# Weight buffers moved to multiples of 512 bytes, and layer 1's expert router fed with rows that are not yet normalised

## The chip, the core and the metric

The kernel is one program on one core of a Trainium2 chip. The metric is device time in microseconds (us) of one execution; lower is better. The profiles come from the hardware profiler of one execution.

## The reference, cut to what matters

Two layers over 256 latent rows and 256 context rows of 1024 columns. Each layer normalises, runs three token mixers, merges them, and then sends every row through a mixture of 32 experts. The layer that matters here is the second (`last`), where only the 256 latent rows are left:

```python
x = layer_norm(DEEPNORM_ALPHA * x + g1 * y_lat, ln1_g[l], ln1_b[l])
h = layer_norm0(x) * (1.0 + sc2) + sh2                     # modulate(x, sh2, sc2)
g_logits = h @ w_rg + b_rg                                 # 4 groups
e_logits = h @ w_re + b_re                                 # 32 experts
# top-1 group, top-2 experts in it, gates from two softmaxes
y = sum over the two experts of gate * ((silu(h @ w1[e]) * (h @ w3[e])) @ w2[e])
x = layer_norm(DEEPNORM_ALPHA * x + g2 * y, ln2_g[l], ln2_b[l])
```

`layer_norm0(x)` is `(x - mean) * r` with `r = 1/sqrt(var + eps)`. All is float32. An expert's three matrices are 6 MiB, so a layer's experts are 201 MB that have to come from HBM once.

## The kernel before, in words

Rows stand in tiles of 128: four tiles in layer 0, two in layer 1 (`T`). The order of the instructions on each engine is made by a list scheduler from the program order (an earlier line has the higher priority; `with self.later(n)` puts a block off by n places).

**Buffers.** SBUF is cut into pools that stand behind one another in each partition. From the left: constants and small tiles (`cp`, `sm`, `lp`), then `wp` (18 buffers of 4 KiB: `raw`, `whi`, `wlo`, `h4`), `rp` (what the router keeps), and then a pool that changes with the stage: `mg` for the mixers, `eg` for the experts, which has six buffers of 8 KiB (tag `ew`) for expert weights. From the right end: `mp` for the mixers and, in its place, `ep` for the experts, which has five more buffers of 8 KiB in layer 1 and three in layer 0 (`ewb`). Four pairs of 4 KiB buffers of `wp` serve in layer 1 as further expert buffers (`self.spare`), so the ring there has 6 + 4 + 5 = 15 places of 1 MiB over all partitions. In the compiled program of before, the first byte of the `wp` buffers lies 128 past a multiple of 512, of the `eg` buffers 64 past one, of all in the right-hand pools 480 past one. One row of a transfer goes to one partition; a weight transfer has 128 rows of 8 KiB, or of 4 KiB into a half of a spare pair.

**Between the merges and the experts** (`out_norm`). The sum of the three branches is split into two float32r parts (`yh`, `yl`) and multiplied by `w_out` (`wo`, 48 matmuls for a tile of rows). Tile by tile follow `norm1` (the first layer norm, which gives `x1`), then `norm2`: `norm0` (mean and variance by `bn_stats` on VectorE, L300, then one ScalarE pass, L320), `logits` (eight PE transposes, L1162; eight modulating copies of 128x128, L1168 on ScalarE and L1170 on VectorE; eight matmuls with the router's 36 columns, L1172) and `top2` on VectorE (from L1211 on). `h2_done` transposes the modulated rows back (L1137) and splits them into `h2hi` and `h2lo` (L817, L818). In layer 1 `h2_done` of the last tile stands behind `route` (`LAST[1]` is 0).

**The experts.** `route` makes slots out of the choices; `one_hot` makes the matrices `OH`, `O1`; `gather_T` multiplies the `h2` parts by `OH` (L1395) and copies the result to `XT` (L1397); `body` multiplies `XT` by `w1` and `w3` (L1525), `tail` by `w2` (L1425), `combine` adds up. Expert weights are loaded on SyncE's queue (L1487) in the order in which they are used. The first six loads of a layer stand behind `left.close()`: they overlay `mg`, whose last readers are the `wo` matmuls. The `ewb` loads overlay `mp`, whose last reader in layer 1 is the `h2_done` behind `route`.

Of the kernel before, what the change touches and what calls it, by code (L numbers as in the profile page):

```python
# [10 lines left out]
F32 = mybir.dt.float32  # L11
F32R = mybir.dt.float32r
# [3 lines left out]
AF = mybir.ActivationFunctionType  # L16
ALU = mybir.AluOpType
# [6 lines left out]
EPS = 1e-6  # L24
# [66 lines left out]
QUICK = (4, 2)  # L91
WARM = 0, 8
HB = (), ()
LAST = 1, 0
NE2 = 3, 2
NC2 = 0, 3
NCT = 2, 2
# [152 lines left out]
class _Prog:  # L250
# [808 lines left out]
    def row(self, ap, tag):  # L1059
        r = self.t([128, 1024], tag, name="row")  # L1060
        self.nc.sync.dma_start(r, ap.to_broadcast([128, 1024]))
        return r

    def out_norm(self, l, T, src):

        nc = self.nc
        nq = 128 * T
        yh, yl = [], []
        for dp in range(4):
            h, lo = self.t([128, 2, 512], "h4", F32R, "yh"), self.t([128, 2, 512], "h4", F32R, "yl")  # L1070
            y = self.y[dp][:, :, :nq]
            nc.scalar.activation(h[:, :, :nq], y, AF.Copy, scale=0.5)
            nc.vector.scalar_tensor_tensor(lo[:, :, :nq], y, 0.5, h[:, :, :nq].bitcast(F32), op0=ALU.mult, op1=ALU.subtract)
            yh.append(h)
            yl.append(lo)
        u, g1 = [], {}
        for t in range(T):
            x = self.t([128, 1024], "o4", name="u")
            nc.sync.dma_start(x, src[t])
            nc.scalar.activation(x, x, AF.Copy, scale=ALPHA)  # L1080
            u.append(x)
        early, late = ("o4", "y4") if l else ("y4", "y4")
        if l:
            g1[0] = self.mod_row(l, "g1", 0, early)
            lg = self.row(self.a["ln"][l, 0:1, :], early)
        first, total = {}, {}
        self.x1 = []

        def norm1(t):
            self.x1.append(self.t([128, 1024], "raw", name="x1"))  # L1090
            if t >= T - QUICK[l]:
                total[t] = self.norm_quick(u[t], self.x1[t], lg, lb)
                first[t] = lambda: None
            else:
                first[t] = self.norm(u[t], u[t], lg, lb, self.x1[t])

        def norm2(t):
            first[t]()
            h = self.t([128, 1024], "o4", name="h2")
            self.norm0(self.x1[t], h, total[t] if t in QS[l] else None)  # L1100
            self.logits(l, t, h)

        w = {(h, q): self.piece(l, ("wo", h, q), ("whi", "wlo") if 2 * q + h < NW[l] else ("g4", "g4")) for q in range(4) for h in range(2)}
        for s in range(len(g1), T // 2):
            g1[s] = self.mod_row(l, "g1", s, late)
            if s == 0:
                lg = self.row(self.a["ln"][l, 0:1, :], late)
        lb = self.row(self.a["ln"][l, 1:2, :], late)
        for t in range(T):
            ts = slice(128 * t, 128 * t + 128)  # L1110
            for h in range(2):
                p = self.ps("wo")
                for k in range(8):
                    s = slice(512 * (k % 2), 512 * (k % 2) + 512)
                    self.mm3(p, yh[k // 2][:, k % 2, ts], yl[k // 2][:, k % 2, ts], w[h, k // 2][0][:, s], w[h, k // 2][1][:, s], k == 0, k == 7)
                hs = slice(512 * h, 512 * h + 512)
                tmp = self.t([128, 512], "b2", name="tmp")
                nc.vector.tensor_tensor(tmp, p, g1[t // 2][:, hs], op=ALU.mult)
                (nc.vector if t >= T - QUICK[l] else nc.gpsimd).tensor_tensor(u[t][:, hs], u[t][:, hs], tmp, op=ALU.add)
            norm1(t)  # L1120
            norm2(t)
            if t % 2 and t < T - 1:
                self.top2(l, t - 1, t + 1, T)
            if t:
                self.h2_done(l, t - 1)
        if LAST[l]:
            self.h2_done(l, T - 1)
        self.top2(l, T - 2, T, T)

# [18 lines left out]
    def logits(self, l, t, h):  # L1148
# [22 lines left out]
        for k in range(8):  # L1171
            mm(self.pl[:, 36 * t:36 * t + 36], hT[:, k], self.wr[:, 36 * k:36 * k + 36], start=k == 0, stop=k == 7)  # L1172

    def warm(self, n, x, name="warm"):

        w = x.shape[-1]
        p = self.ps(name)
        with self.later(5000):
            for i in range(n):
                self.nc.tensor.matmul(p[:w, :256], x, self.c["iota"], start=True, stop=True)  # L1180


    def top2(self, l, t0, t1, T):

        nc, c = self.nc, self.c
        TT, TS, STT, RED = nc.vector.tensor_tensor, nc.vector.tensor_scalar, nc.vector.scalar_tensor_tensor, nc.vector.tensor_reduce
        if t0 == 0:
            self.brt = self.t([128, 36], "u1", name="brt")
            nc.sync.dma_start(self.brt, self.a["brt"][l:l + 1, :].to_broadcast([128, 36]))
            x = self.t([128, 1024], "whi", name="route")  # L1190
            self.lg, self.oh = x[:, 0:144], x[:, 144:400]
            g = self.rp.tile([128, 3, T], F32, name=f"gates{l}", tag="gates")
            self.gt = [g[:, i] for i in range(3)]

            self.g2p = self.rp.tile([128, T, 2], F32R, name=f"g2p{l}", tag="g2p")
            self.gdp = self.rp.tile([128, T, 3], BF, name=f"gdp{l}", tag="gdp")
            self.scr, self.scr2 = [x[:, 512 + 128 * i:640 + 128 * i] for i in range(2)], x[:, 768:1024]
            self.M = self.t([128, 32 * T], "u1", BF, "M")
        n = t1 - t0
        lg = self.lg[:, 36 * t0:36 * t1].rearrange("p (t e) -> p t e", e=36)  # L1200

        def row(x, w):
            return x[:, None, :].to_broadcast([128, n, w])
# [4 lines left out]
        def tiles(x):  # L1208
            return x[:, 32 * t0:32 * t1].rearrange("p (t e) -> p t e", e=32)

        TT(lg, self.pl[:, 36 * t0:36 * t1].rearrange("p (t e) -> p t e", e=36), row(self.brt, 36), op=ALU.add)  # L1211

        def mark(oh, x, m, weights, w, op=ALU.is_equal):

# [20 lines left out]
        with self.later():  # L1235
# [12 lines left out]
            p, q = self.g2p[:, t0:t1], self.gdp[:, t0:t1]  # L1248
# [132 lines left out]
        for t in range(T):  # L1381
            mm(p[:, 2:5], O1[:, t], self.gdp[:, t], start=t == 0, stop=t == T - 1)

    def gather_T(self, OH, w, T):

        nc, mm = self.nc, self.nc.tensor.matmul
        XT = self.t([128, 8, w], "e8", name="XT")
        per = 512 // w
        for i in range(0, 8, per):
            p = self.ps("XT")  # L1390
            for j in range(per):
                k = i + j
                for t in range(T):
                    for part in range(2):
                        mm(p[:, w * j:w * j + w], self.h2s[t][part][:, 128 * k:128 * k + 128], OH[:, t], start=t == 0 and part == 0,  # L1395
                           stop=t == T - 1 and part == 1)
            (nc.scalar.copy if (i // per) % 2 else nc.vector.tensor_copy)(XT[:, i:i + per], p.rearrange("p (a b) -> p a b", b=w))  # L1397
        return XT

# [89 lines left out]
    def experts(self, l, T):  # L1489
        nc, mm, c = self.nc, self.nc.tensor.matmul, self.c  # L1490
# [5 lines left out]
        XTs, gates, CY, held = {}, {}, {}, {}  # L1496

        def front(dp):
            d = self.slot
            if dp:  # L1500
                d = self.small(2 * T)
                nc.vector.tensor_scalar(d, self.slot, -256.0 * dp, None, op0=ALU.add)
            OH, O1 = self.one_hot(c["iota"], 256, T, d)
            XTs[dp] = self.gather_T(OH, 256, T)
            pg = self.ps("gate")
            for pr in range(2):
                ss = slice(128 * pr, 128 * pr + 128)
                self.slot_gates(pg[:, 8 * pr:8 * pr + 5], OH[:, :, ss], O1[:, :, ss], T)
            gates[dp] = self.small(2)
            nc.vector.tensor_reduce(gates[dp], pg[:, 0:16].rearrange("p (a b) -> p a b", a=2)[:, :, 0:5], axis=AX.X, op=ALU.add)  # L1510
            CY[dp] = []
# [44 lines left out]
    def overflow(self, l, T):  # L1556

        nc, mm, c = self.nc, self.nc.tensor.matmul, self.c
# [8 lines left out]
        with self.tc.For_i(0, nblk, 1):  # L1567
            sel, eq, row = self.small(1), self.small(16), self.small(1)
# [10 lines left out]
            nc.vector.tensor_scalar(sel, cnt, 128.0, None, op0=ALU.mult)  # L1579
            nc.vector.tensor_scalar(d, self.over, sel, None, op0=ALU.subtract)  # L1580
            OH, O1 = self.one_hot(c["iota"][:, :128], 128, T, d)
            XT = self.gather_T(OH, 128, T)
            pg = self.ps("gate")
            self.slot_gates(pg[:, 0:5], OH, O1, T)
            gate = self.small(1)
# [58 lines left out]
    def run(self):  # L1644
        nc, a = self.nc, self.a
        self.md, self.mT, self.mT2, self.nraw = {}, {}, {}, {}
        self.setup()
        self.rp = self.ctx.enter_context(self.tc.tile_pool(name="rp", bufs=1))
        self.x2 = [self.dr.tile([128, 1024], F32, name=f"x2_{t}") for t in range(2)]
        src = [a["x"][0:128], a["x"][128:256], a["cx"][0:128], a["cx"][128:256]]  # L1650
        xs = None
        for l in range(NL):
# [37 lines left out]
                self.modulation(1, [0], "ew")  # L1690
            self.load(l, us, 0, range(4), most=6)
            self.route(l, T)
            if not LAST[l]:
                self.h2_done(l, T - 1)

            tags = ("raw", "h4", "h4", "wx") if l else ("wx",)
            self.spare = [[self.t([128, 1024], ("whi", "wlo")[v] if tag == "wx" else tag, name="ew") for v in range(2)] for tag in tags]
            right.close()
            right = self.open("ep", "right", [("ewb", RNG[l]), ("e8", 2), ("g2", T // 2), ("oh", 1), ("o1", 1), ("e2", NE2[l]), *([("c2", NC2[l])] if l else []), ("ct", NCT[l]), ("row", 2)])

            self.sums = [self.cp1(f"sum{t}", 2) for t in range(T)]
            self.experts(l, T)
            if l:
                lgb = self.final_loads(l)
# [38 lines left out]
```

## Time and profile before

| | us |
|---|---|
| median of 3 runs | 2134.95 |
| lowest and highest of them | 2132.41, 2136.12 |
| the profiled execution | 2129.76 |
| its span, first to last instruction | 2128.0 |
| TensorE busy in it | 1964.5 |
| VectorE, ScalarE, GpSimd busy | 956.0, 569.4, 259.9 |

A matmul is written down from its start to its modelled end, so that neighbours overlap and a busy TensorE is not one at its peak. The profile moves 562.40 MB by DMA, mean 264 GB/s. The mixers of layer 0 take about the first 640 us, its experts run to about 1140, the mixers of layer 1 to about 1610, its experts to about 2106; then comes the last norm.

### The profile page before, as it was taken

The page shows a single profiled execution, that of the slowest core. Times are in us where ns is not written, and L with a number is a line of the kernel's source. Part 1 is how long each engine was busy: PE and PEld are TensorE (multiplying, and loading weights), DVE is VectorE, ACT ScalarE, POOL GpSimd, SP SyncE. Part 2 cuts the span into 40 slices and gives each one's busy share as a digit, 9 for nine tenths or more (in the row PEclk, how much of TensorE's full clock was granted, in tenths as well). Part 3 has the DMA queues.
Part 4 walks back from the last instruction along what each step waited for, and adds up shares of the span by engine and source line. Part 5 has one row for each costly group of instructions (what it writes and reads, how often), then busy time and mean ns, then how long its engine had stood idle before and what let it go on. Part 6 is the DMA issues. An engine that isn't in the chain of part 4 may idle for free. (4 is left out here: it accounts for less than half of the span.)

```text
span 2128.0 us, 28181 instructions
## 1 busy us (share of the span) xinstructions
PE 1964.5 (92%) x10749; PEld 1183.4 (56%) x10749; DVE 956.0 (45%) x2275; ACT 569.4 (27%) x1008; POOL 259.9 (12%) x259
## 2 busy tenths in 40 slices
PE   5999999999998998999899698999996999999986
PEld 1676777777885352545253275977895443343332
DVE  4676766464387130222122765776557122222113
ACT  3443344343233000000000454444452101100001
POOL 1322100011110010111011122100020000000000
PEclk9999999999999999999999898999997999999998
DMA  7436222223329899999998734533476999999996
GB/s 294 159 132 218 75 68 73 95 85 103 123 79 380 348 420 419 403 406 419 419 402 339 283 95 138 182 109 102 130 232 268 408 416 418 418 416 419 416 418 245
DMA packets 116435, 562.40 MB, mean 264 GB/s; under 512 B 13575, under 2 KB 15111, under 8 KB 76745
## 3 DMA queue, kind: packets, MB, share of 16 engines
q1 hardware_dynamic: 115720, 558.85, 68.1%
q8 instruction: 87, 1.43, 0.3%
q10 hardware_dynamic: 576, 1.70, 0.2%
q14 instruction: 52, 0.42, 0.1%
HBM read 557.36 MB, written 3.15 MB: 263 GB/s over the span
## 5 line engine op out<-in xcount | busy, mean ns | idle before, releaser
L1525 PE MATMUL h<-ew,XT 128*64 128x512 f32 (+2 forms) x2048 | 478.3, 613 | 29.1 <-DMA ew<-in_ew_dram 29.0
L1525 PEld LDWEIGHTS h<-ew,XT 128*64 128x64 f32 (+2 forms) x2048 | 150.0, 135 | 311.9 <-issue 250.5
L1425 PE MATMUL Y<-ew,aT 128*64 128x512 f32 (+2 forms) x1024 | 250.5, 597 | 11.3 <-DMA ew<-in_ew_dram 6.1
L292 DVE TENSOR_TENSOR wlo<-raw,whi 128x1024 fp32r<-128x1024 f32 (+1 forms) x140 | 179.0, 1279 | 133.6 <-ACT whi L291 132.6
L1447 POOL TENSOR_TENSOR x<-x,ct 128x512 f32<-128x512 f32 x76 | 96.5, 1298 | 933.2 <-DVE ct L1442 636.8
L380 PE MATMUL pT<-hThi,whi 128*128 128x512 f32 (+1 forms) x576 | 203.6, 353 | 2.2 <-DVE zq L880 1.4
L291 ACT CAST whi<-raw 128x1024 fp32r<-128x1024 f32 (+1 forms) x140 | 145.4, 1039 | 224.9 <-PE pT L381 126.8
L382 PE MATMUL pT<-hThi,wlo 128*128 128x512 f32 (+1 forms) x576 | 202.5, 352 | 0.2 <-DVE wlo L292 0.2
L381 PE MATMUL pT<-hTlo,whi 128*128 128x512 f32 (+1 forms) x576 | 202.2, 351 | 0.0
L1415 DVE SCALAR_TENSOR_TENSOR act<-h,s,act 128x512 f32<-128x512 f32 x30 | 22.5, 750 | 317.5 <-PE h L1525 273.8
L1425 PEld LDWEIGHTS Y<-ew,aT 128*64 128x64 f32 (+2 forms) x1024 | 77.5, 133 | 148.5 <-issue 119.7
L818 DVE TENSOR_TENSOR Yl<-Y,Yh 128x512 fp32r<-128x512 f32 x60 | 41.5, 691 | 261.5 <-ACT Yh L817 259.7
L817 ACT CAST Yh<-Y 128x512 fp32r<-128x512 f32 x60 | 35.2, 586 | 420.0 <-PE Y L1425 413.9
L380 PEld LDWEIGHTS pT<-hThi,whi 128*128 128x128 f32 x576 | 110.0, 191 | 22.9 <-ACT whi L291 4.5
L382 PEld LDWEIGHTS pT<-hThi,wlo 128*128 128x128 f32 x576 | 109.8, 191 | 16.3 <-issue 2.6
L381 PEld LDWEIGHTS pT<-hTlo,whi 128*128 128x128 f32 x576 | 110.1, 191 | 14.4 <-issue 1.9
L380 PE MATMUL pM<-whi,hThi 128*128 128x512 f32 (+1 forms) x304 | 110.4, 370 | 2.1 <-DVE zkv L858 1.7
L381 PE MATMUL pM<-wlo,hThi 128*128 128x512 f32 (+1 forms) x304 | 111.4, 367 | 0.0
L382 PE MATMUL pM<-whi,hTlo 128*128 128x512 f32 (+1 forms) x304 | 111.1, 366 | 0.0
L495 PE MATMUL mod<-wmod,sT 128*32 128x512 f32 x320 | 73.9, 625 | 22.2 <-DVE s L343 14.5
L1419 ACT COPY aT<-aT 128x512 f32<-128x512 f32 x30 | 17.6, 586 | 283.8 <-PE aT L1418 283.8
L1395 PE MATMUL XT<-OH,h2hi 128*128 128x256 f32 x352 | 88.9, 290 | 0.0
(373 smaller groups left out, 3084.9 us busy)
## 6 DMA issues: line engine op xcount, KB each, us to landing
ew<-in_ew_dram SPq DMA_DIRECT2D x309, 1024.0 KB, 16.2
ew<-in_ew_dram SPq DMA_DIRECT2D x150, 512.0 KB, 13.8
raw<-in_w_dram SPq DMA_DIRECT2D x145, 512.0 KB, 3.7
wmod<-in_wmod_dram SPq DMA_DIRECT2D x96, 512.0 KB, 6.2
nb<-in_nb_dram SPq DMA_DIRECT2D x32, 256.0 KB, 3.8
g<-md SPq DMA_DIRECT2D x12, 256.0 KB, 11.2
row<-in_ln_dram SPq DMA_DIRECT2D x4, 512.0 KB, 5.2
lgb<-in_ln_dram SPq DMA_DIRECT2D x4, 512.0 KB, 7.8
```

The source lines that it names most:

```text
L291: self.nc.scalar.copy(hi, src)
L292: (eng or self.nc.vector).tensor_tensor(lo, src, hi.bitcast(F32), op=ALU.subtract)
L380: mm(out, lh, rh, start=start, stop=False)
L381: mm(out, lh, rl, start=False, stop=False)
L382: mm(out, ll, rh, start=False, stop=stop)
L495: nc.tensor.matmul(p[32 * j:32 * j + 32, :], self.sT[:, k, :], raws[j // 2][:, 512 * (j % 2):512 * (j % 2) + 512], start=k == 0, stop=k == 7)
L817: self.nc.scalar.copy(hi, src)
L818: self.nc.vector.tensor_tensor(lo, src, hi.bitcast(F32), op=ALU.subtract)
L1395: mm(p[:, w * j:w * j + w], self.h2s[t][part][:, 128 * k:128 * k + 128], OH[:, t], start=t == 0 and part == 0, stop=t == T - 1 and part == 1)
L1425: mm(y[m * i:m * i + m, :], aT[:, 128 * f + m * i:128 * f + m * i + m], w2(f, n, i), start=f == 0, stop=f == 3)
L1447: nc.gpsimd.tensor_tensor(self.x1[t][:, ns], self.x1[t][:, ns], tmp, op=ALU.add)
L1525: mm(h[m * i:m * i + m, :], XTs[dp][:, k, 128 * pr + m * i:128 * pr + m * i + m], w[i, 2 * q + k // 4][k % 4], start=k == 0, stop=k == 7)
```

## The change

Three things are changed together.

1. A tile of 480 bytes at the right end (`edge`) shifts everything in the right-hand pools; the tiles `sum0` to `sum3` of 32 bytes each leave `lp`, and one tile of 64 bytes (`sums`) joins `rp`. With the sizes as they are, the buffers of `wp`, `eg`, `mg`, `mp` and `ep` then begin at multiples of 512.
2. In layer 1 the logits are made from the rows `x1` themselves. With `r` and `b = -mean * r` of a row, the logits are `r * (x1 @ (s * w_r)) + b * (column sums of s * w_r) + (shift @ w_r + bias)`, where `s` is `1 + scale`. `router` makes the scaled weights, the column sums and the shifted bias once, after the last tile of `yh` is there (two copies of one element order its loads behind it); `raw_logits` transposes `x1` and multiplies; `top2` puts the three terms together. `h2_rows` makes mean, variance and the two parts of the normalised rows without any modulation and without transposing back.
3. The modulation is done in `gather_T` for layer 1, on the gathered and transposed slots, while they are copied out of PSUM.

```diff
-LAST = 1, 0
...
         def norm2(t):
             first[t]()
+            if l and t == 0:
+                self.router(l, yh[3])
+            if l:
+                self.raw_logits(l, t)
+                self.h2_rows(l, t, total[t])
+                return
...
-            if t:
+            if t and l == 0:
                 self.h2_done(l, t - 1)
-        if LAST[l]:
+        if l == 0:
             self.h2_done(l, T - 1)
...
+    def router(self, l, after):
+        nc, mm = self.nc, self.nc.tensor.matmul
+        wr, wa = self.t([128, 288], "u2", name="wr"), self.t([128, 8, 36], "u2", name="wra")
+        nc.vector.tensor_copy(wr[0:32, 0:1], after[0:32, 0, 0:1].bitcast(F32))
+        nc.sync.dma_start(wr, self.a["wr"][l])
+        self.brt = self.t([128, 36], "u1", name="brt")
+        nc.vector.tensor_copy(self.brt[0:32, 0:1], after[0:32, 0, 0:1].bitcast(F32))
+        nc.sync.dma_start(self.brt, self.a["brt"][l:l + 1, :].to_broadcast([128, 36]))
+        self.pl, self.h2s, self.rb, self.wra = self.ps("logit"), [], {}, wa
+        nc.vector.tensor_tensor(wa, wr.rearrange("p (k e) -> p k e", e=36), self.mT2[l][:, 0, 0, :][:, :, None].to_broadcast([128, 8, 36]), op=ALU.mult)
+        for k in range(8):
+            mm(self.pl[:, 144:180], self.c["one"][:, 0:1].to_broadcast([128, 128]), wa[:, k], start=k == 0, stop=k == 7)
+        for k in range(8):
+            mm(self.pl[:, 180:216], self.mT2[l][:, 1, 0, k:k + 1].to_broadcast([128, 128]), wr[:, 36 * k:36 * k + 36], start=k == 0, stop=k == 7)
+        nc.vector.tensor_tensor(self.brt, self.brt, self.pl[:, 180:216], op=ALU.add)
+
+    def raw_logits(self, l, t):
+        nc, mm = self.nc, self.nc.tensor.matmul
+        xT = self.t([128, 8, 128], "o4", name="xT")
+        for i in range(2):
+            p = self.ps("h2T")
+            for k in range(4):
+                nc.tensor.transpose(p[:, 128 * k:128 * k + 128], self.x1[t][:, 512 * i + 128 * k:512 * i + 128 * k + 128], self.ident)
+            (nc.scalar.copy if i else nc.vector.tensor_copy)(xT[:, 4 * i:4 * i + 4], p.rearrange("p (a b) -> p a b", a=4))
+        for k in range(8):
+            mm(self.pl[:, 36 * t:36 * t + 36], xT[:, k], self.wra[:, k], start=k == 0, stop=k == 7)
+
+    def h2_rows(self, l, t, total):
+        nc = self.nc
+        st = self.small(20)
+        nmu, v, b = st[:, 0:1], st[:, 1:2], st[:, 2:3]
+        x, h = self.x1[t], self.t([128, 1024], "o4", name="h2")
+        nc.vector.tensor_scalar(nmu, total, -1.0 / 1024, None, op0=ALU.mult)
+        nc.scalar.activation(h, x, AF.Square, bias=nmu, accum_out=v)
+        nc.vector.tensor_scalar(v, v, 1.0 / 1024, EPS, op0=ALU.mult, op1=ALU.add)
+        r = self.rsqrt(v, 1, st[:, 3:6])
+        nc.vector.tensor_tensor(b, nmu, r, op=ALU.mult)
+        self.rb[t] = r, b
+        hi, lo = self.t([128, 1024], "h4", F32R, "h2hi"), self.t([128, 1024], "h4", F32R, "h2lo")
+        nc.scalar.activation(h, x, AF.Identity, bias=b, scale=r)
+        nc.scalar.activation(hi, x, AF.Identity, bias=b, scale=r)
+        with self.later(60):
+            for i in range(2):
+                ns = slice(512 * i, 512 * i + 512)
+                nc.vector.tensor_tensor(lo[:, ns], h[:, ns], hi[:, ns].bitcast(F32), op=ALU.subtract)
+        self.h2s.append((hi, lo))
...
-        TT(lg, self.pl[:, 36 * t0:36 * t1].rearrange("p (t e) -> p t e", e=36), row(self.brt, 36), op=ALU.add)
+        if l:
+            for t in range(t0, t1):
+                x, (r, b) = self.lg[:, 36 * t:36 * t + 36], self.rb[t]
+                STT(x, self.pl[:, 144:180], b, self.brt, op0=ALU.mult, op1=ALU.add)
+                STT(x, self.pl[:, 36 * t:36 * t + 36], r, x, op0=ALU.mult, op1=ALU.add)
+        else:
+            TT(lg, self.pl[:, 36 * t0:36 * t1].rearrange("p (t e) -> p t e", e=36), row(self.brt, 36), op=ALU.add)
...
+            if l:
+                for j in range(per):
+                    sc, sh = (self.mT2[l][:, n, 0, i + j:i + j + 1] for n in range(2))
+                    if (i + j) % 2:
+                        nc.scalar.activation(XT[:, i + j], p[:, w * j:w * j + w], AF.Identity, bias=sh, scale=sc)
+                    else:
+                        nc.vector.tensor_scalar(XT[:, i + j], p[:, w * j:w * j + w], sc, sh, op0=ALU.mult, op1=ALU.add)
+                continue
...
+        edge = self.ctx.enter_context(self.tc.tile_pool(name="edge", bufs=1, side="right")).tile([128, 120], F32, name="edge")
+        nc.vector.memset(edge, 0.0)
...
-            if not LAST[l]:
-                self.h2_done(l, T - 1)
...
-            self.sums = [self.cp1(f"sum{t}", 2) for t in range(T)]
+            sums = self.rp.tile([128, 16], F32, name=f"sums{l}", tag="sums")
+            self.sums = [sums[:, 2 * t:2 * t + 2] for t in range(T)]
```

## Rows read from the trace of the kernel before

**Rows 1.** The page's part 2: DMA rate in 40 slices of 53 us.

```profile
GB/s 294 159 132 218 75 68 73 95 85 103 123 79 380 348 420 419 403 406 419 419 402 339 283 95 138 182 109 102 130 232 268 408 416 418 418 416 419 416 418 245
```

**Rows 2.** Windows: length; busy (count) by engine; PEclk, DMA share, GB/s.

```profile
730.00:1128.00 398.00, 372.64 (x1855) 169.87 (x1856) 84.05 (x143) 30.81 (x54) 50.41 (x40) 0.97 1.00 413
...
1690.00:2050.00 360.00, 346.34 (x1594) 139.73 (x1592) 77.26 (x125) 36.31 (x63) 30.65 (x24) 1.00 1.02 417
...
2100.00:2106.00 6.00, 5.22 (x23) 1.89 (x24) 0.25 (x1) 1.17 (x2) 0.00 (x0) 1.00 0.63 253
```

**Rows 3.** The same view where layer 1's experts begin.

```profile
1614.00:1623.00 9.00, 2.52 (x12) 2.47 (x12) 8.90 (x36) 2.82 (x4) 0.00 (x0) 0.50 1.01 427
1623.00:1634.00 11.00, 8.20 (x46) 7.82 (x46) 6.36 (x24) 6.42 (x12) 0.00 (x0) 0.66 0.97 378
...
1637.50:1642.00 4.50, 4.50 (x15) 2.75 (x14) 4.38 (x33) 1.18 (x3) 0.00 (x0) 0.50 0.38 102
...
1645.00:1650.50 5.50, 5.50 (x48) 5.00 (x48) 4.79 (x16) 1.76 (x3) 0.00 (x0) 1.00 1.01 429
1650.50:1665.00 14.50, 14.50 (x73) 6.45 (x70) 1.65 (x4) 1.29 (x2) 0.00 (x0) 1.00 0.98 379
```

**Rows 4.** Timeline of SyncE's queue, from the mixers' last loads to the experts'.

```profile
1587.92 4.68 SPq L373 DMA_DIRECT2D raw<-in_w_dram  x3
1609.35 7.74 SPq L1487 DMA_DIRECT2D ew<-in_ew_dram  x10
...
1640.18 18.27 SPq L1487 DMA_DIRECT2D ew<-in_ew_dram  x9
```

**Rows 5.** Waits of SyncE's queue, 1605 to 1660: us, times, longest.

```profile
SPq L1487 <- PE h2b L1137: 10.5, 1, 10.5
```

**Rows 6.** Timeline of TensorE, 1595 to 1700: start, length, instructions.

```profile
1608.93 0.39 PE L381 MATMUL wo<-g,yh 128*128 128x512 f32 x1
1609.16 0.40 PE L382 MATMUL wo<-g,yl 128*128 128x512 f32 x1
1620.48 1.97 PE L1162 MATMUL h2T<-cst,h 128*128 128x128 f32 x8 [10.92 <-ACT h L320]
1622.24 3.93 PE L1172 MATMUL logit<-wr,h2T 128*128 128x36 f32 x16
...
1645.19 0.36 PE L1395 MATMUL XT<-OH,h2hi 128*128 128x256 f32 x1
...
1649.68 14.00 PE L1525 MATMUL h<-ew,XT 128*64 128x512 f32 x64
```

**Rows 7.** Timeline of VectorE, 1611 to 1650.

```profile
1611.68 1.28 DVE L355 SCALAR_TENSOR_TENSOR x<-u,s,row 128x1024 f32<-128x1024 f32 x1
...
1619.07 1.28 DVE L355 SCALAR_TENSOR_TENSOR x<-u,s,row 128x1024 f32<-128x1024 f32 x1
...
1631.65 0.23 DVE L1211 TENSOR_TENSOR route<-logit,brt 128x72 f32<-128x72 f32 x1 [0.70 <-PE logit L1172]
```

**Rows 8.** Instructions by line, 1600 to 1665: busy us, mean ns.

```profile
L280 DVE TENSOR_SCALAR s<-s 128x1 f32<-128x1 f32 x12 | 3.0, 268 | 0.1
...
L818 DVE TENSOR_TENSOR h2lo<-h2b,h2hi 128x512 fp32r<-128x512 f32 x4 | 2.8, 690 | 0.6 <-ACT h2hi L817 0.4
...
L300 DVE BATCH_NORM_STATS2 s<-x 128x6 f32<-128x512 f32 x4 | 2.6, 686 | 0.1
...
L320 ACT ACTIVATE h<-x,s 128x1024 f32<-128x1024 f32 x2 | 2.5, 1240 | 22.4 <-DVE s L319 22.4
```

**Rows 9.** Timeline of TensorE in layer 0, 636 to 700.

```profile
640.96 1.42 PE L1172 MATMUL logit<-wr,h2T 128*128 128x36 f32 x12
```

**Rows 10.** Windows in steady running, by the buffers that are filled (columns as above).

```profile
1721.00:1729.00 8.00, 8.00 (x39) 3.15 (x40) 5.05 (x10) 0.70 (x2) 2.24 (x2) 1.00 1.01 418
...
1811.00:1819.00 8.00, 8.00 (x41) 2.75 (x38) 0.00 (x0) 1.08 (x2) 0.00 (x0) 1.00 1.02 423
...
1825.00:1830.50 5.50, 5.50 (x38) 4.04 (x38) 2.58 (x5) 1.17 (x2) 2.53 (x2) 1.00 1.02 408
```

More of the change, by code (lines that the diff above doesn't have):

```diff
@@ L1187, in top2 @@
         if t0 == 0:
-            self.brt = self.t([128, 36], "u1", name="brt")
-            nc.sync.dma_start(self.brt, self.a["brt"][l:l + 1, :].to_broadcast([128, 36]))
+            if l == 0:
+                self.brt = self.t([128, 36], "u1", name="brt")
+                nc.sync.dma_start(self.brt, self.a["brt"][l:l + 1, :].to_broadcast([128, 36]))
             x = self.t([128, 1024], "whi", name="route")
@@ L1382, in slot_gates, with gather_T @@
             mm(p[:, 2:5], O1[:, t], self.gdp[:, t], start=t == 0, stop=t == T - 1)
-    def gather_T(self, OH, w, T):
+    def gather_T(self, l, OH, w, T):
         nc, mm = self.nc, self.nc.tensor.matmul
@@ L1503, in front @@
             OH, O1 = self.one_hot(c["iota"], 256, T, d)
-            XTs[dp] = self.gather_T(OH, 256, T)
+            XTs[dp] = self.gather_T(l, OH, 256, T)
             pg = self.ps("gate")
@@ L1581, in overflow @@
             OH, O1 = self.one_hot(c["iota"][:, :128], 128, T, d)
-            XT = self.gather_T(OH, 128, T)
+            XT = self.gather_T(l, OH, 128, T)
             pg = self.ps("gate")
```

## The prediction, made before the changed kernel ran

> **What bounds the kernel now.** I read the slices first, for the stages: in slices 13 to 21 and 32 to 39 the DMA engines move 348 to 420 GB/s, and these are the two expert stages; the mixers between them mostly run at a third of that [rows 1]. Then the windows, which put numbers on it: over 360 us in the middle of layer 1's experts the DMA share is 1.02 at 417 GB/s, over 398 us of layer 0's 1.00 at 413, and the last transfers run out by about 2106 [rows 2]. What comes behind 2106 (2128.0 - 2106 = 22 us of last products and norm) hangs on the last transfer and is not touched. So in layer 1 the end is: the moment the loads begin, plus bytes over rate, plus holes in the stream, plus 22 us. Only three things can move it: an earlier or later begin, fewer holes, a higher rate.
>
> The begin and the holes: SyncE's queue issues the first expert load at 1609.35 [rows 4], when the last `wo` matmul starts its last 0.40 us [rows 6]; TensorE's last product of the mixers releases the buffers. The windows that follow show full flow at 427, then 378, then a hole of 4.5 us at 102 GB/s, 429 for 5.5 us, and 379 for 14.5 us [rows 3]. Behind the hole stands a wait of 10.5 us of SyncE's queue for the back transposes [rows 5], and the nine loads behind it begin at 1640.18 [rows 4]: the right-hand buffers are free only when the `h2b` transposes behind `route` are done. The weak 14.5 us follow because the first expert product starts at 1649.68 [rows 6], later than the 15 places of the ring were ordered.
>
> **The holes, and what the new router takes from the way to them.** At 417 GB/s the two holes cost 4.5 * (1 - 102/417) = 3.4 us and 14.5 * (1 - 379/417) = 1.3 us, together 4.7 us. The window at 378 holds the gate rows' small packets; it stays.
>
> Before, the second tile's `x1` is ready at 1619.07 + 1.28 = 1620.35, and the router's chain can begin only at 1631.65 [rows 7], 11.3 us later: two `bn_stats` (2 * 0.69, [rows 8]), small operations (0.27 each with their gaps, [rows 8]), the ScalarE pass of 1.24, transposes, modulating copies, matmuls. In the changed kernel the transposes start from `x1` itself: 1.97 us for eight [rows 6] at the low level of the clock (granted 0.50, 1.2 GHz, after TensorE idled behind `wo` [rows 3, 6]), a copy of 512 columns (0.69, the length of VectorE's operation on 512 columns from PSUM, L818 in [rows 8]), eight matmuls 3.93/2 = 1.97 [rows 6], together about 4.6 us. Beside them run the squares (1.24, as the ScalarE pass of the same size, [rows 8]) and about nine small operations (9 * 0.27 = 2.4), together 3.7, so the statistics are hidden behind the transposes; if they are not, at most 1 us shows. Two `bn_stats` of the first tile leave VectorE ahead of the second tile's `x1`: 1.3 us. Four small operations take the place of one (L1211, 0.23) at the head of `top2`: 3 * 0.2 = 0.6 us back. So the choices begin 11.3 - 4.6 + 1.3 - 0.6, say 7 us earlier, counted from the end of `wo`. The two parts of the rows (two ScalarE passes of 1.24, two subtractions of 0.69 a tile) are needed only at the gather and have the 5 us of `top2` as cover; without it they would cost 2.6 us. The back transposes and their copies, which stood between the slots and the gather, are gone. The modulation on gathered slots replaces one copy of 512 columns per bank by two of 256, one on each of VectorE and ScalarE: no longer for the first front, and later fronts lie behind transfers; at nothing.
>
> With the first gather at about 1638 instead of 1645.19 [rows 6], the ten loads first issued fill the DMA engines until about 1637.5 [rows 3], and the right-hand buffers are free by then, since their last readers are now the subtractions. I count both holes as closed: **-4.7 us**. Bounds: 0 if the subtractions come as late as the transposes did, -5.7 if the window at 378 gains its 1 us too.
>
> **What the router's set-up costs.** Sixteen matmuls of 36 columns, two VectorE copies of one column, two loads, two small VectorE operations. They are ready when the last `yh` is there, at about 1592, when the last mixer loads are just out [rows 4] and TensorE works through `wo` without a gap; they stand ahead of the second tile's `wo` in the program's order. Layer 0 shows such matmuls among others at 1.42/12 = 0.12 us each [rows 9]: 16 * 0.12 = **+1.9 us** on the end of `wo`, and the first expert load moves with it. Bounds: 0 if they are put into the 10.92 us in which TensorE stands idle behind `wo` [rows 6]; 16 * 3.93/16 = 3.9 us if each takes what it takes at the low clock. The two loads stand on SyncE's queue behind a VectorE copy that waits for `yh`; behind them stand at most the last three `raw` loads, which begin at 1587.92 [rows 4], and who waits for those is `wo`. I take nothing for it, and up to 2 us for the range.
>
> **What the alignment is worth.** No row shows a transfer into a buffer at a multiple of 512, so I bound it. Below, nothing: with the offsets of before the stream does reach 427 and 429 GB/s [rows 3], and in steady running the right-hand buffers (offset 480) are filled at 418 and the left-hand ones (offset 64) at 423 [rows 10], a difference within what such windows scatter by. Above: the steady rate rises to the best one shown, 427. That would be 450 us * 10/427 = 10.5 us in layer 1 (1650 to 2100) and 398 * (427 - 413)/427 = 13.0 us in layer 0, 23.5 us together. A loss I exclude: no transfer gets more bytes or packets. I take a quarter of the gap in layer 1 (2.6 us) and, as layer 0's stream is also held up by buffers that TensorE has still to read, an eighth there (1.6 us): **-4.2 us**, near the lower end, since the two offsets shown do not differ by much. Half-buffers (offset 128, rows of 4 KiB) run at 408 [rows 10]; they keep their packet size.
>
> A rule speaks against any gain. The Trainium skill (DMA: Bandwidth & Descriptors, "Why small descriptors are slow" and "Where 436 GB/s comes from") gives each packet a fixed overhead of about 3 cycles beside 32-byte beats and a ceiling of 435 GB/s; an estimate from it for rows of 8 KiB is 435 * 256/259 = 430 GB/s. The trace's 427 and 429 at unaligned offsets [rows 3] are already there; by this rule the term is 0 and the sum -2.8 us.
>
> **The sum** against the profiled execution: 2129.76 + 1.9 - 4.7 - 4.2 = 2122.8. The median of the runs stands 2134.95 - 2129.76 = 5.2 us above it, so 2128.0 us, 0.33% under the median. What a measurement of this kernel can tell from no change is about 0.2%, 4.3 us.
>
> **Rivals.** *The steady rate rises to the calm one.* For it: 427 and 429 were reached, with an empty ring as the only visible difference; against it: at the same offsets as the 418. Layer 1 gives its 10.5 us, layer 0 perhaps half of its 13.0, and with the front's -2.8 that is 2134.95 - 2.8 - 17 = 2115. A page's rule would bring this about: the Trainium skill (DMA: Bandwidth & Descriptors, "How a descriptor splits into AXI transactions") has a descriptor that does not start at a multiple of 256 bytes pay beats from the multiple below; by it an estimate is 2 beats of 256 at offset 64, 7 at 480 and 4 of 128 for the half rows, some 2% over the ring. The trace does not bear out its order: offset 480 should be 2% slower than 64, and the windows give 418 and 423, half of that, with scatter.
>
> *The alignment does nothing.* Then only the front is left: 2134.95 - 2.8 = 2132.1, which can't be told from no change. For it: the calm rates at unaligned offsets.
>
> *Slower: a transpose of the first tile stands in TensorE's queue ahead of `wo` matmuls of the second.* Before, that tile's transposes wait until 1620.48 for the norm [rows 6]. Now they need only `x1`, which is ready at 1611.68 + 1.28 = 1612.96 [rows 7], 3.4 us behind the last `wo`; in program order they come first. If the planner thinks VectorE a little faster than it is, TensorE waits at them with `wo` matmuls behind it, and the expert loads with these. With a half of the second tile's products behind (24 that start 0.23 apart [rows 6], 5.6 us), the eight transposes and eight matmuls at full clock (2.0) and the set-up, `wo` ends at 1613 + 2.0 + 5.6 = 1620.6 instead of 1609.5: +11 us, less 4.7, or 2141. It decides from about ten matmuls behind the first transpose on. Against it: in the trace of before nothing of the first tile's norm stands inside `wo`.
>
> **How the numbers follow.** The forecast (a small gain in rate, holes closed, 2121 to 2132) 0.40; the calm rate 0.20; no effect of alignment 0.22; slower 0.18. Faster by over 0.2%: 0.36 of the forecast, 0.20, and 0.04 of the third, together 0.60; within 0.2%: 0.04, 0.17 and 0.02, 0.23; slower: 0.16 and 0.01, 0.17. The likeliest alone has 2121 to 2132. For 8 in 10 the range reaches down to the calm rate, 2113, and up to 2139, short of the full price of the slower case.
>
> **What would show it.** Windows in steady running at 420 or a little over (right), 417 (third case), 427 (first). The set-up's sixteen matmuls inside `wo`, and the first expert load about 2 us later against the end of the merges. `top2` some 7 us nearer to the end of `wo`; no wait of SyncE's queue for TensorE before the ring is full; no window near 100 GB/s between 1637 and 1642 of the old count. Wrong: a raw transpose ahead of `wo` matmuls; the subtractions behind the slots, with a hole as before; a steady rate outside 417 to 427.

## The result, and the profile after

The changed kernel takes 2115.66 us (median of four runs, 2113.1 to 2118.37) against 2133.68 us of the kernel before (four runs, 2130.98 to 2136.12): ratio 0.9916, 95% interval 0.9896 to 0.9936. It is faster, by 18 us. The forecast of 2128 had the sign and the closing of the holes right; the gain is two to three times as large, and most of what is missing belongs to the alignment.

The profile page's GB/s by slice, of the changed kernel, answers to [rows 1]: slices of the expert stages that stood at 416 to 420 are at 424 to 426.

```profile
GB/s 296 154 139 222 72 70 73 95 86 95 132 81 383 349 426 426 406 406 425 426 400 341 286 96 130 182 121 93 133 221 256 425 424 425 424 424 425 424 425 240
```

Windows of the changed kernel (columns as in [rows 2]): the beginning of layer 1's experts in pieces, its first 51.5 us as one, and the steady stretch.

```profile
1604.50:1613.00 8.50, 3.13 (x26) 2.81 (x25) 8.12 (x29) 2.63 (x3) 0.00 (x0) 0.83 0.91 355
1613.00:1622.00 9.00, 5.34 (x24) 4.79 (x23) 6.54 (x25) 6.51 (x9) 0.00 (x0) 0.50 1.00 419
1622.00:1630.00 8.00, 4.44 (x15) 2.58 (x16) 7.49 (x51) 0.40 (x2) 0.00 (x0) 0.50 1.02 386
1630.00:1636.00 6.00, 6.00 (x43) 5.07 (x42) 6.00 (x23) 0.63 (x2) 0.00 (x0) 0.96 1.03 400
1636.00:1642.00 6.00, 6.00 (x36) 2.56 (x36) 2.20 (x7) 2.70 (x4) 0.00 (x0) 1.00 1.00 425
1642.00:1656.00 14.00, 14.00 (x86) 8.26 (x85) 3.71 (x9) 2.85 (x5) 0.00 (x0) 1.00 1.01 426
1604.50:1656.00 51.50, 38.91 (x224) 26.06 (x224) 34.04 (x141) 15.72 (x23) 0.00 (x0) 0.80 1.00 404
...
1670.00:2030.00 360.00, 348.73 (x1608) 138.97 (x1610) 84.41 (x139) 43.03 (x76) 30.57 (x24) 1.00 1.02 425
```

The hole at 102 GB/s and the weak stretch at 379 of [rows 3] are gone: the DMA share stays at 0.91 or more throughout. The same first 51.5 us in the kernel before, counted from its own first expert load:

```profile
1609.50:1661.00 51.50, 34.91 (x184) 24.34 (x185) 35.34 (x144) 13.86 (x23) 0.00 (x0) 0.73 0.92 363
```

At the old steady rate the difference is 51.5 * (404 - 363)/417 = 5.1 us, with a little of the new rate in it. The timeline of SyncE's queue in the changed kernel, against [rows 4], and its waits from 1600 to 1655, against [rows 5] (us in total, times, longest):

```profile
1579.69 4.68 SPq L372 DMA_DIRECT2D raw<-in_w_dram  x3
1585.83 0.33 SPq L1187 DMA_DIRECT2D wr<-in_wr_dram  x1
1586.21 0.42 SPq L1190 DMA_DIRECT2D brt<-in_brt_dram  x1
1604.35 16.49 SPq L1561 DMA_DIRECT2D ew<-in_ew_dram  x13
1622.95 1.55 SPq L528 DMA_DIRECT2D g<-md  x2
1625.68 6.48 SPq L1561 DMA_DIRECT2D ew<-in_ew_dram  x6
```

```profile
SPq L1561 <- DMA ew<-in_ew_dram: 19.6, 13, 3.6
SPq L1561 <- PE h L1599: 13.8, 5, 7.3
SPq L1561 <- PE wo L381: 13.7, 1, 13.7
```

The wait of 10.5 us for the back transposes does not appear. The one on `h` is the ordinary one for a place in a full ring. The router's two loads stand behind the last `raw` loads and hold up nothing.

TensorE's timeline of the changed kernel, against [rows 6]:

```profile
1593.28 0.39 PE L379 MATMUL wo<-g,yh 128*128 128x512 f32 x1
1593.51 0.31 PE L1194 MATMUL logit<-wra,cst 128*128 128x36 f32 x2
1593.65 0.47 PE L380 MATMUL wo<-g,yh 128*128 128x512 f32 x1
...
1594.89 1.64 PE L1194 MATMUL logit<-wra,cst 128*128 128x36 f32 x14
1596.36 1.95 PE L1196 MATMUL logit<-wr,mU 128*128 128x36 f32 x16
1598.15 0.48 PE L379 MATMUL wo<-whi,yh 128*128 128x512 f32 x1
...
1604.16 0.40 PE L381 MATMUL wo<-g,yl 128*128 128x512 f32 x1
1604.39 1.04 PE L1206 MATMUL h2T<-cst,x 128*128 128x128 f32 x8
...
1612.77 1.94 PE L1206 MATMUL h2T<-cst,x 128*128 128x128 f32 x8 [4.27 <-DVE x L354]
1615.32 3.63 PE L1209 MATMUL logit<-wra,xT 128*128 128x36 f32 x16 [0.61 <-DVE xT L1207]
...
1632.12 0.36 PE L1460 MATMUL XT<-OH,h2hi 128*128 128x256 f32 x1
```

The set-up is inside `wo`, as forecast, but as 2 + 14 + 16 = 32 instructions. The `wo` matmuls around them start 0.23 us apart; the set-up puts 0.14 us (1593.51 to 1593.65) and 3.26 us (1594.89 to 1598.15) between them, 3.4 us together, 0.106 us for one. The first tile's transposes come right behind the last `wo`, with no idle time ahead of them. VectorE's timeline, against [rows 7]:

```profile
1611.33 1.28 DVE L354 SCALAR_TENSOR_TENSOR x<-u,s,row 128x1024 f32<-128x1024 f32 x1
...
1618.98 0.26 DVE L1273 SCALAR_TENSOR_TENSOR route<-logit,s,brt 128x36 f32<-128x36 f32 x1 [1.29 <-PE logit L1209]
...
1620.37 1.29 DVE L1229 TENSOR_TENSOR h2lo<-h,h2hi 128x512 fp32r<-128x512 f32 x2
```

From the second tile's `x1` (1611.33 + 1.28) to the head of `top2` it is 6.4 us instead of 11.3; the statistics are hidden, since the wait ahead of 1618.98 is for the logits. The first gather starts 27.6 us behind the end of `wo` (1604.16 + 0.40 to 1632.12) instead of 35.6 (1609.16 + 0.40 to 1645.19).

### The profile page after: what moved, and what is told of

The parts are those of the page before. It is cut to its first block, busy times and chain, and to the rows that moved or that the text cites. A ratio compares the mean times of both kernels' runs of the same rounds, so it can differ in the third digit from the quotient of the medians.

```text
span 2111.2 us, 28236 instructions
## 1 busy us (share of the span) xinstructions
PE 1959.1 (93%) x10765; PEld 1182.6 (56%) x10765; DVE 961.7 (46%) x2289; ACT 577.6 (27%) x1020; POOL 257.7 (12%) x259
```

## The experiments

Two theories stood against each other for the larger gain. *Address*: where a transfer's row begins in a partition sets its rate. *Stream*: the rate rises because the front no longer leaves holes behind. The table has every run. The runs from "alignment only" to "set-up behind `wo`" were timed beside 2132.08 of the kernel before, the four below them beside 2130.35 on another chip, the last two, one execution each, beside 2128.61 on a third, and the changed kernel's first ratio goes by 2133.68. The median and the ratio are timed, the last four columns are read from the one profiled execution of each. "Layer 0" is from the start of the first `h` product of its experts to the start of the last, "`wo`" from the first to the last start of layer 1's `wo` matmuls, "load to end" the time from its first expert load to the end of the span.

| kernel | median us | ratio, interval | steady GB/s | layer 0 | `wo` | load to end |
|---|---|---|---|---|---|---|
| before | 2133.68, 2132.08, 2130.35, 2128.61 | | 417 | 468.2 | 22.1 | 518.6 |
| changed | 2115.66 | 0.9916, 0.9896 to 0.9936 | 425 | 464.6 | 25.2 | 506.9 |
| alignment only | 2119.09 | 0.9938, 0.992 to 0.9955 | 425 | 466.4 | 21.6 | 510.2 |
| router only | 2131.8 | 1.0, 0.9989 to 1.0012 | 417 | 468.1 | 25.6 | 514.2 |
| at 256 past | 2116.28 | 0.9927, 0.991 to 0.9943 | 425 | 466.3 | 25.2 | 506.3 |
| set-up behind `wo` | 2112.75 | 0.9908, 0.9891 to 0.9924 | 425 | 464.2 | 21.6 | 506.4 |
| the same, old offsets | 2126.16 | 0.9986, 0.9975 to 0.9997 | 417 | 468.3 | 22.0 | 513.9 |
| at 128 past | 2125.37 | 0.9975, 0.9964 to 0.9985 | 418 | 467.4 | 25.3 | 513.4 |
| changed, again | 2115.16 | 0.9936, 0.992 to 0.9953 | 425 | 464.2 | 25.2 | 506.9 |
| set-up behind `wo`, again | 2112.45 | 0.9916, 0.9901 to 0.993 | 425 | 465.3 | 21.6 | 506.5 |
| left aligned only, one execution | 2115.16 | | 424 | 466.8 | 25.2 | 507.5 |
| right aligned only, one execution | 2121.97 | | 421 | 466.6 | 25.7 | 510.1 |

**Alignment only.** The kernel before with the edge tile and the one tile of sums; the router stays.

```diff
+        edge = self.ctx.enter_context(self.tc.tile_pool(name="edge", bufs=1, side="right")).tile([128, 120], F32, name="edge")
+        nc.vector.memset(edge, 0.0)
...
-            self.sums = [self.cp1(f"sum{t}", 2) for t in range(T)]
+            sums = self.rp.tile([128, 16], F32, name=f"sums{l}", tag="sums")
+            self.sums = [sums[:, 2 * t:2 * t + 2] for t in range(T)]
```

> The kernel before with the edge tile and the one sums tile alone, so that every weight buffer begins at a multiple of 512; the router is the old one. Theory 'address' (the multiple itself shortens the rows' transfers): steady windows at 425 GB/s as in the changed kernel, layer 0's experts about 4 us and layer 1's about 8 us shorter, and whatever the mixers gained with it; ratio 0.993 to 0.995, 2120 to 2125 us. Rival 'stream' (the new front starts the stream without a hole, and that keeps the rate up): steady 417, ratio 1.000.

**Router only.** The changed kernel with those lines taken back.

> The changed kernel with the old offsets (64, 128, 480): new router and modulation, no alignment. 'Address': steady 417; the hole of 3.4 us and the weak 1.3 us are closed and the set-up in the products of w_out costs 3.9 us (32 instructions at 0.12), so ratio 0.998 to 1.000. Rival 'stream': steady 425 and ratio 0.992.

Windows of the alignment alone, then of the router alone: the first 51.5 us of the expert loads, and the steady stretch, for which the kernel before has 417 in the same window.

```profile
1604.20:1655.70 51.50, 34.91 (x188) 24.53 (x189) 35.13 (x144) 13.87 (x23) 0.00 (x0) 0.77 0.93 370
1670.00:2030.00 360.00, 350.83 (x1624) 140.74 (x1622) 78.69 (x127) 36.89 (x64) 30.60 (x24) 1.00 1.02 425
```

```profile
1610.50:1662.00 51.50, 38.91 (x224) 26.08 (x224) 34.04 (x141) 15.73 (x23) 0.00 (x0) 0.80 0.99 402
1670.00:2030.00 360.00, 344.19 (x1588) 136.67 (x1586) 82.92 (x136) 42.83 (x75) 30.68 (x24) 1.00 1.02 417
```

Each part moves one of the two numbers and nearly leaves the other. With the hole still there (370) the alignment reaches 425; with the hole closed (402) the old offsets stay at 417. "Address" holds, and "stream" falls. One size was missed: about 4 us were expected in layer 0's experts, and 468.2 - 466.4 = 1.8 came.

The traces also hold the time of each DMA packet, which in these loads is one row of a transfer. Over the same 360 us the loads keep the engines as busy after as before, but move more (packets, MB, share of the time of 16 engines, over 1670 to 2030 us; before, then changed):

```profile
q1 hardware_dynamic: 26357, 149.97, 101.4%
q1 hardware_dynamic: 26187, 152.68, 101.3%
```

A row of 8 KiB takes 314.7 ns on average before and 309.4 in the changed kernel, a row of 4 KiB 162.7 and 159.3. Of the 8 KiB rows 92% take more than 309 ns before and in the router alone, 0.2% in the changed kernel and in the alignment alone. So in this stretch the rows themselves got shorter; it is not that gaps between them were closed.

**At 256 past a multiple of 512**, all weight buffers, to tell 512 from 256:

```diff
-        edge = self.ctx.enter_context(self.tc.tile_pool(name="edge", bufs=1, side="right")).tile([128, 120], F32, name="edge")
+        edge = self.ctx.enter_context(self.tc.tile_pool(name="edge", bufs=1, side="right")).tile([128, 56], F32, name="edge")
         nc.vector.memset(edge, 0.0)
+        nc.vector.memset(self.cp1("pad", 64), 0.0)
```

> The changed kernel with all weight buffers 256 past a multiple of 512. If a multiple of 256 is enough: steady 425 and the changed kernel's ratio, 0.992. If it has to be 512: steady 417 to 418 and the ratio of the new router alone, 0.998 to 1.000.

**At 128 past**, in the same way (an edge of 88 columns, a pad of 32).

> The changed kernel with every weight buffer moved to 128 bytes past a multiple of 512 (left and right). Theory 'only a multiple of 256 counts' (writes go out in pieces that end at multiples of 256): the gain of alignment falls away, steady windows at about 417 GB/s, about 2131 us, ratio 0.999 to 1.000. Rival 'a multiple of 128, or of 64, is enough on its own and the bad ones were 480 and the mixture of offsets': 425 GB/s and about 2116 us, ratio 0.992 to 0.993. In between (about 421 GB/s, 2123 us) the price would grow with the distance from a multiple of 256.

The steady windows of the one at 256, then of the one at 128:

```profile
1670.00:2030.00 360.00, 348.72 (x1610) 138.73 (x1608) 84.45 (x139) 43.41 (x76) 30.63 (x24) 1.00 1.02 425
```

```profile
1670.00:2030.00 360.00, 344.30 (x1594) 137.06 (x1592) 82.88 (x136) 42.78 (x75) 30.62 (x24) 1.00 1.02 418
```

256 is as good as 512, and 128 is nearly as bad as the old mixture; of the 8 KiB rows 0.1% and 76% take more than 309 ns. The time of the one at 128 was missed: about 2131 us were expected. The 2125.37 are 5 us under the kernel before, with an interval (0.9964 to 0.9985) clear of that of the router alone (0.9989 to 1.0012), to which its rate and its stages are nearly alike. The two were timed on different chips, between which the changed kernel itself went from 0.9916 to 0.9936; where the 5 us come from is not shown. Beside it on the same chip the changed kernel is 10.2 us faster.

**Left or right alone**, one execution each: the changed kernel without the edge, and with the edge but the four old `sum` tiles.

> The changed kernel with the buffers on the left (`wp`, `eg`, `mg`) at multiples of 512 and those on the right back at 480 past one. In layer 1 ten of the ring's fifteen places are then good. Theory 'each transfer pays for its own offset, about alike for each bad one': two thirds of the way from 417 to 425, a steady rate of about 422 GB/s. Rival 'the right-hand offset 480 is the whole price': 417. Rival 'the left-hand ones, 64 and 128, are the whole price': 425.

> The mirror of the run before: the right-hand buffers at multiples of 512, the left-hand ones back at 64 (`eg`) and 128 (`wp`). Theory 'each transfer pays for its own offset': a third of the way, about 420 GB/s. If 480 is the whole price: 425; if 64 and 128 are: 417.

Steady windows, left aligned only, then right aligned only:

```profile
1670.00:2030.00 360.00, 347.53 (x1606) 139.42 (x1604) 84.45 (x139) 43.42 (x76) 30.66 (x24) 1.00 1.02 424
```

```profile
1670.00:2030.00 360.00, 345.65 (x1598) 138.33 (x1594) 82.97 (x136) 43.33 (x76) 30.66 (x24) 1.00 1.02 421
```

Neither class is the whole price. The ten places on the left cost 4 GB/s (425 to 421) when they alone are bad, the five on the right 1 (425 to 424); together they cost 8, so the two don't simply add. Both runs came out above what "each transfer pays for its own offset" gave (424 against 422, 421 against 420). Which offset is dearer for one place can't be read from them: on top of the other class the left costs 7 (424 to 417) and the right 4 (421 to 417), and the left has twice the places.

The packets show part of why. With the right-hand places bad, five of the eleven for 8 KiB rows, only 15% of these rows take more than 309 ns, and they come in bursts: from 1710 to 1715 us none, from 1717 to 1720 between 51 and 96% of each microsecond's rows, and the next burst begins at about 1754, one turn of the ring later (15 MiB at 424 GB/s, 37 us). So a bad offset did not lengthen every row; what decides when it does is not shown.

**The set-up behind `wo`.** `norm2` calls `router` and both tiles' `raw_logits` only for the last tile, so that no set-up matmul stands ahead of the second tile's `wo` in the program's order.

```diff
...
-            if l and t == 0:
-                self.router(l, yh[3])
             if l:
-                self.raw_logits(l, t)
+                if t == T - 1:
+                    self.router(l, yh[3])
+                    for s in range(T):
+                        self.raw_logits(l, s)
                 self.h2_rows(l, t, total[t])
...
```

> The changed kernel with the router's set-up and the first tile's raw logits in the program behind the second tile's w_out products. If the set-up costs its 32 matmuls where the changed kernel has them: w_out ends 3.5 to 4.5 us earlier counted from its begin, the loads of layer 1 start as much earlier, and all of it reaches the end: ratio 0.990, 2112 us. If the choices are now late (set-up, transposes and logits between 1600 and 1607 ahead of the second tile): the hole comes back, and the ratio stays at 0.992.

> The new router with its set-up called behind the second tile's `wo` (last tile) and the old offsets of the buffers. Theory: with the set-up inside `wo` the front's gain (about 4.7 us of closed holes) was paid back by the 3.1 us the set-up takes, which is why the router alone gave 1.000; without that price the router alone should give about 3 to 4 us, 2128 to 2129 against about 2132 (ratio 0.998), with `wo` of layer 1 at about 22 us and steady windows at 417 GB/s. Rival (the front gives nothing because the stream is behind for another reason, and the better version's 2112.75 was scatter of the chip): 2132, ratio 1.000.

> The changed kernel itself, once more, as the measure for the next one on the same chip: 2114 to 2117 us, ratio 0.991 to 0.993; steady windows at 425 GB/s, `wo` of layer 1 at 25.2 us.

> The changed kernel with the router's set-up behind the second tile's `wo`, once more, beside the changed kernel on the same chip. Theory 'the set-up inside `wo` costs its whole 3.1 us, since the expert loads start behind it': 3 us under the changed kernel's median (about 2112.5 to 2113.5 us), ratio to the kernel before 0.9905 to 0.991, first expert load 3 to 4 us earlier. Rival 'the closed hole absorbs it': within 1 us of the changed kernel.

TensorE's timeline with the set-up behind `wo`:

```profile
1600.37 0.39 PE L381 MATMUL wo<-g,yl 128*128 128x512 f32 x1
1600.60 1.87 PE L1197 MATMUL logit<-wra,cst 128*128 128x36 f32 x16
1602.30 2.30 PE L1199 MATMUL logit<-wr,mU 128*128 128x36 f32 x16
1604.57 1.94 PE L1209 MATMUL h2T<-cst,x 128*128 128x128 f32 x8
...
1611.64 1.94 PE L1209 MATMUL h2T<-cst,x 128*128 128x128 f32 x8 [1.28 <-DVE x L354]
1614.49 3.63 PE L1212 MATMUL logit<-wra,xT 128*128 128x36 f32 x16 [0.91 <-DVE xT L1210]
```

`wo` is back at 21.6 us, and, counted from its first matmul, the second tile's logits come no later: the set-up now lies in time in which TensorE waited. In the second pair, too, the first expert load comes 3.6 us earlier, counted so. With the new offsets the median is 2.7 us under that of the changed kernel beside it (2112.45 against 2115.16, with 3 expected; the intervals of their ratios still meet); 2112.45 and 2112.75 are the lowest medians found.

With the old offsets this router measured 4.2 us under the kernel before (0.9975 to 0.9997), where the router with its set-up in `wo` gave nothing on another chip. That does not show what the place of the set-up is worth: on the chip of the 4.2 us the run at 128, with its set-up in `wo`, gained 5.0. The profiles show the move itself: `wo` takes 22.0 us instead of 25.6, and load to end stays (513.9 against 514.2).

## Why the prediction was right in sign and short in size

**The step that failed** is the price of the alignment: "I take a quarter of the gap in layer 1 (2.6 us)" and "an eighth there (1.6 us)" for layer 0, "near the lower end, since the two offsets shown do not differ by much." Measured alone the alignment is worth 13.0 us (2132.08 to 2119.09), not 4.2. In the profiles 518.6 - 510.2 = 8.4 us of it lie between layer 1's first expert load and the end, where 2.6 were forecast, and 468.2 - 466.4 = 1.8 in layer 0's experts (3.6 in the changed kernel), where 1.6 were. So the term that was mis-sized is layer 1's: the steady rate made nearly the step that the first rival gave, 417 to 425 instead of 427. The argument was unsound: 418 and 423 in [rows 10] were two bad offsets, and two bad ones that are alike say nothing about a good one. Nor did the 427 and 429 of [rows 3] show that a bad offset costs nothing. In these two windows 0.4% and none of the 8 KiB rows take more than 309 ns, in the steady stretch 92%: short windows behind the beginning of the stream and behind the hole do not show the steady price.

A rule spoke for this, and I gave the rival that it stands behind 0.20. The Trainium skill (DMA: Bandwidth & Descriptors, "How a descriptor splits into AXI transactions") has a descriptor that does not begin at a multiple of 256 bytes pay for the bytes below. The runs at 256 (425) and at 128 (418) agree with it on the write side in SBUF, and 425/417 = 1.019 agrees with the estimate of some 2%. The prediction held against it that the windows do not bear out its order; but 418 at 480 and 423 at 64 are in its order, at half its size. By this rule, with the prediction's beats over the fifteen places, an estimate is 1.1% for the left-hand places and 0.9% for the right-hand ones. Measured alone they cost 0.9% (421) and 0.2% (424), so the right-hand ones fall short of it.

The rule that I set against it is from the same page of the Trainium skill (DMA: Bandwidth & Descriptors, "Why small descriptors are slow" and "Where 436 GB/s comes from"): a ceiling, with an estimate of 430 GB/s for these rows. The 425 stays under it; the step from it to no gain failed.

That 2115.66 lies in the range is owed to its lower end, which was put at the first rival's time; the likeliest case alone had 2121 to 2132. That this rival's 2115 is so near is in part luck: half of 13.0 us in layer 0 and 2.8 at the front were too much (1.8 to 3.6, and 0.9 in the router alone), and the profile's gain has 4.6 us that no term holds.

**The holes**: -4.7 forecast. The router alone shortens load to end by 518.6 - 514.2 = 4.4 us, with old offsets and the set-up moved 4.7. Right. Of the path to it, "say 7 us earlier" became 8 us at the gather (35.6 - 27.6); the cover of the subtractions held.

**The set-up**: +1.9 forecast; 25.6 - 22.1 = 3.5 us in the router alone. The price of one instruction (0.12, [rows 9]) was about right, the count was not: each of the sixteen calls is two instructions. [Rows 6] had shown it, x16 for one tile's eight calls, and I took half of that row's time for eight; the changed kernel's 3.63 for eight calls shows that mistake too. Holes and set-up nearly cancel, 3.5 - 4.4 = -0.9 where -2.8 was forecast, and the router alone measures 1.0.

**The rivals.** "The alignment does nothing" and the slower case fell. The first tile's transposes stand behind the last `wo` (1604.39) and waited for nothing. (The 1620.6 of the slower case leaves out the set-up that it names.)

**What stays open.** Set-up, holes, rate and layer 0 explain, for the changed kernel, (506.9 - 518.6) + (25.2 - 22.1) + (464.6 - 468.2) = -12.2 us of the profiled execution's -16.8; 5.3 of the rest lie ahead of layer 0's experts, whose first product starts at 686.3 instead of 691.6. The router alone, with the old offsets, has 687.8, and two executions of the kernel with the set-up behind `wo` have 686.7 and 691.6. So one execution against another can't tell whether the alignment gives something to layer 0's mixers too. The medians leave room as well: the two parts alone add up to 13.3 us (13.0 and 0.3), the changed kernel measured 18.0 and, again, 15.2.

## What to carry to other kernels

Let every buffer that is filled by long DMA rows begin at a multiple of 256 bytes in its partition, and look at the compiled addresses after any change of a small tile: here a shift by some hundred bytes was worth more than a new router. When a rate has the same value at every offset that a trace shows, all of them can be bad; try the good one before pricing it, and don't take the steady price from windows just behind a pause. Count instructions, not calls, when work is put into a stage that holds back a stream, and put it where that engine waits anyway.

## What was not expected of the hardware

The loads of 8 KiB and 4 KiB rows into SBUF run at 425 GB/s over 360 us when their destinations begin at multiples of 256 or 512, and at 417 to 418 at 128 or at a mixture of 64, 128 and 480; bad places on the left alone give 421, on the right alone 424. At good offsets 99.8% or more of the 8 KiB rows take no more than 309 ns; at bad offsets they do so too in the windows of [rows 3] at 427 and 429 GB/s, but take 314 to 315 on average in the steady stretch. A call of an f32 matmul of 36 columns appears as two instructions, 0.106 us each at a granted clock of 1.00 (2.4 GHz) between other matmuls (32 of them, 3.4 us).
